# Neighbourhood attention in pairs: negated scores, keys in eight pieces, gate loads with the scores, two copies off ScalarE

## The chip, the cores and the metric

The kernel runs on one core of a Trainium2 chip. The metric is the device time of one execution in microseconds (us); three runs of the kernel before gave 1550.53, 1550.68 and 1553.64 us, so the median is 1550.68 us. All data are float32. Products use a split of one factor, or of both, into a high and a low part (`hh`/`hl`, `wh`/`wl`), each of which is kept in the form that the rows call fp32r.

## What is computed

There are two layers over 1024 latent tokens (a grid of 16 rows by 64 columns) and 256 context tokens, with 1024 features. Each layer normalises the input, projects it, runs three mixers side by side, multiplies each by a SiLU gate and projects back. The part that the change touches is the third mixer, attention of each grid row to a band of 8 rows and 16 columns, with a bias table, and to all context tokens:

```python
def row_block(r):
    r0 = jnp.clip(r - kh // 2, 0, rows - kh)
    ...
    s_nb = jnp.einsum("bqhd,bmqnhd->bhqmn", q_r, k_nb).astype(jnp.float32)
    bias = rpb[:, drow[:, None, None], dcol[None, :, :]]
    s_nb = s_nb + jnp.transpose(bias, (0, 2, 1, 3)).astype(jnp.float32)[None]
    s_ctx = jnp.einsum("bqhd,bchd->bhqc", q_r, k_ctx).astype(jnp.float32)
    s = jnp.concatenate([s_nb.reshape(bsz, NA_HEADS, GRID_W, n_nb), s_ctx], axis=-1)
    p = jax.nn.softmax(s, axis=-1).astype(v.dtype)
    ...
y = jnp.concatenate([a_out * silu(ag), b_out * silu(bg), n_out * silu(ng)], axis=-1) @ w_out[l]
```

The first mixer is attention of 8 heads over all tokens (grouped keys), the second a pooling mixer. In the first layer the context tokens also attend among themselves, with the heads of the first and of the third mixer.

## The kernel before, in words

A layer goes through these stages: projections (weights split on ScalarE and VectorE, products on TensorE, results written to DRAM as `qnd`, `knd`, `qad`, `kad`, gates as `ngd`, `agc`, `agd`); the **pair stage**, which the change is about; the global attention (lines 957 to 1139); the output projection (from line 1144). In the profiled execution the pair stage runs from about 398 to 523 us in the first layer and from about 1132 to 1237 us in the second.

The pair stage takes units of 128 queries and two heads (`pair_unit`, line 814). A neighbourhood unit (kind "n") of latent tokens has 4 or 5 tiles of 128 neighbourhood keys (`nk`) and two tiles of context keys; units of context queries ("n" with `nk` 0, and kind "c" for heads of the first mixer) have the two context tiles alone. The first layer has 28 units (two head pairs of 8 latent and 2 context units, then 8 "c" units), the second has 16. A unit has four steps:

- `scores(hi)` (line 823), for each of two heads: TensorE writes scores into one of two double banks `ps_w`. VectorE takes the maximum `m` over the 256 context columns (line 834), then one custom instruction adds the bias table in place and carries the maximum on (line 837; its accumulator is read by a second instruction). A small instruction negates the maximum into `nm` (line 841).
- `weights(hi)` (line 844): at the first head the unit's gate (64 KB, `ngate`) is loaded through SyncE's queue (line 847). ScalarE computes the exponential with bias `nm` and the row sum (line 852); VectorE takes the reciprocal `rr` (line 854); GpSimd multiplies the gate by it into `rg` (line 855).
- `transposes(hi)` (line 859), one unit later: TensorE transposes 128x128 blocks of the weights, four to a bank `ps_b` (three banks), at the second head also `rg` as the last block; ScalarE copies each bank to `probt` (line 870).
- `values()` (line 873), two units later: TensorE multiplies by the values (line 877), VectorE multiplies by the transposed gate into `una` (line 880), ScalarE copies that to `hh` (line 806), and GpSimd writes the rest to `hl` (line 807).

In one round of the loop at line 1086 the order on TensorE is: scores of head 0 of unit n, transposes of head 0 of unit n-1, scores of head 1, transposes of head 1, values of unit n-2. In the last 10 units of the first layer and the last 7 of the second, three products for the maxima of the global attention (`shift_step`, lines 985 and 990; they use the same three `ps_b` banks, and VectorE reduces each into `gmx`, line 986) stand in each round too.

TensorE's order is the program's (`manual_schedule`, line 97). On the other engines and on SyncE's queue a scheduler sets the order, by its own estimate of when things are ready; each engine then works its list in that order. All the loads and stores here go through SyncE's one queue.

The stage begins with the keys of the first head pair in `kst`. The keys of the second pair (`na_keys_load(1)`, line 901: four tiles, each loaded twice into halves of 64 partitions, eight transfers of 320 KB) are asked for together before unit 2; they go into `hh` and `hl`, and unit 10 (first layer) or 8 (second) is the first that reads them. `store_u` (line 803) is also used for the pooled branch (`fin`, line 811) and in the global attention.

Of the kernel before, what the change touches and what calls it, by code (L numbers as in the profile page):

```python
# [24 lines left out]
NTT = NT // P  # L25
HD = 64
EPS = 1e-6
NEG = -1e30
PB = 7
QB = 6  # L30

# [43 lines left out]
def hybrid_block_kernel(  # L75
# [84 lines left out]
    def load_gains():  # L160

        for i, g in enumerate((na_k_gain, att_k_gain, att_q_gain, na_q_gain)):
            for hf in range(2):
                SP.dma_start(out=gcol[hf * 64:(hf + 1) * 64, i, :], in_=g.rearrange("l d -> d l"))
        DVE.tensor_scalar(out=gcol[:, 2:4], in0=gcol[:, 2:4], scalar1=0.125, scalar2=None, op0=ALU.mult)

    hh = const.tile([P, KT, NT], F32R, name="hh")
    hl = const.tile([P, KT, NT], F32R, name="hl")
# [203 lines left out]
    for l in range(DEPTH):  # L372
# [391 lines left out]
        def na_table(h):  # L764

            T, I = tab_bufs[h % 2]
            for qr in range(2):
                off = RPB_PAD + (l * 4 + h) * RPB_H + (1 - qr) * 31 + 15
                SP.dma_start(out=T[qr * 64:(qr + 1) * 64],
                             in_=bass.AP(rpbd.tensor, rpbd.offset + off, [[RPB_S - 1, 64], [31, 14], [1, 64]]))  # L770
            DVE.tensor_tensor(out=T, in0=T, in1=cmask.unsqueeze(1).to_broadcast([P, 14, 64]), op=ALU.add)

        def na_inner(h):
            T, I = tab_bufs[h % 2]
            ACT.activation(out=I, in_=T[:, 2:12], func=AF.Copy)
            POOL.memset(I[0:64, 8:10], NEG)
            POOL.memset(I[64:128, 0:1], NEG)
            POOL.memset(I[64:128, 9:10], NEG)

        def load_nq(h, c0, n):  # L780
            t = ak_.tile([P, 512], F32R, name="nq", tag="q", bufs=QB)
# [5 lines left out]
        def na_keys_load(pr):  # L787

            places = [(hh[:, 2 + hi, :], hl[:, 2 + hi, :]) if pr else (kst(), kst()) for hi in range(2)]
            cur["k", pr] = [tuple(load_twice(places[hi][i], knd, 2 * pr + hi, 1 - i) for i in range(2)) for hi in range(2)]  # L790

        def na_q(pr, cc):
            cur["q", pr, cc] = [load_nq(2 * pr + hi, cc * 512, 512 if cc < 2 else 256) for hi in range(2)]

        na_keys_load(0)
        na_q(0, 0)
        for h in range(2):
            na_table(h)
# [4 lines left out]
        def store_u(f, t0, n, u, eng=DVE):  # L803

            dst = hh[:, f, t0:t0 + n]
            ACT.activation(out=dst, in_=u, func=AF.Copy)
            eng.tensor_tensor(out=hl[:, f, t0:t0 + n], in0=u, in1=dst.bitcast(F32), op=ALU.subtract)

        def pool_u(f, t0, n):
# [1 line left out]
            SP.dma_start(out=u[:, :n], in_=upd[f, :, t0:t0 + n])  # L811
            store_u(4 + f, t0, n, u[:, :n])

        def pair_unit(t, f, qs, ks, kbase, vs, k0, nk, tabs, gsrc):

            nl = nk * P
            base = 768 - nl
# [2 lines left out]
            st = _Env()  # L820
            st.s, st.p, st.pt = [None] * 2, [None] * 2, [None] * 2

            def scores(hi):
                q1, q2 = qs(hi)
                k1, k2 = ks[hi]
                S = ps_pair("ps_s")
                segs = [(base, k0 * P, 512 - base), (512, k0 * P + 512 - base, 256)] if nk else []
                segs.append((768, SEQ, 256))
                for o, kc, n in segs:
                    kc -= kbase  # L830
                    PE.matmul(S[:, o:o + n], q1, k1[:, kc:kc + n], start=True, stop=False)
                    PE.matmul(S[:, o:o + n], q2, k2[:, kc:kc + n], start=False, stop=True)
                m = small.tile([P, 1], F32, tag="m2", name="m2")
                DVE.reduce_max(out=m, in_=S[:, 768:1024], axis=AX.X)
                if nk:
                    m1 = small.tile([P, 1], F32, tag="m1", name="m1")
                    DVE.tensor_tensor_reduce(out=S[:, base:768], in0=S[:, base:768], in1=tabs[hi], scale=1.0, scalar=m,
                                             op0=ALU.add, op1=ALU.max, accum_out=m1)
                    m = m1
                nm = small.tile([P, 1], F32, tag="nm", name="nm")  # L840
                DVE.tensor_scalar(out=nm, in0=m, scalar1=-1.0, scalar2=None, op0=ALU.mult)  # L841
                st.s[hi] = S, nm

            def weights(hi):
                if hi == 0:
                    st.gate = ap_.tile([P, P], F32, name="ngate", bufs=3)
                    SP.dma_start(out=st.gate, in_=gsrc)
                    st.rg = ap_.tile([P, P], F32, name="rg", bufs=3)
                S, nm = st.s[hi]
                p = ap_.tile([P, 1024], F32, name="prob", tag="prob", bufs=PB)  # L850
                sm = small.tile([P, 1], F32, tag="sm", name="sm")
                ACT.activation(out=p[:, base:1024], in_=S[:, base:1024], func=AF.Exp, bias=nm, accum_out=sm)  # L852
                r = small.tile([P, 1], F32, tag="rr", name="rr")
                DVE.reciprocal(out=r, in_=sm)
                POOL.tensor_scalar(out=st.rg[:, hi * 64:(hi + 1) * 64], in0=st.gate[:, hi * 64:(hi + 1) * 64], scalar1=r,
                                   scalar2=0.0, op0=ALU.mult, op1=ALU.add)
                st.p[hi] = p

            def transposes(hi):

                p = st.p[hi]
                blocks = [p[:, base + i * P:base + (i + 1) * P] for i in range(nt)] + ([st.rg] if hi else [])
                pt = ap_.tile([P, 1024], F32, name="probt", tag="prob", bufs=PB)
                for i0 in range(0, len(blocks), 4):
                    part = blocks[i0:i0 + 4]
                    T = ps_one("ps_t")
                    for i, b in enumerate(part):
                        PE.transpose(T[:, i * P:(i + 1) * P], b, ident)  # L868
                    o = pt[:, i0 * P:(i0 + len(part)) * P]
                    ACT.activation(out=o, in_=T[:, :len(part) * P], func=AF.Copy)  # L870
                st.pt[hi] = pt

            def values():
# [16 lines left out]
        def early(i, fn):  # L890
            before.setdefault(max(i, 0), []).append(fn)

        order = [0, 1, 6, 7, 4, 5, 2, 3] + list(range(NTL, ntq))
        for pr in range(2):
# [33 lines left out]
        def make_unit(kind, pr, t):  # L928
            if kind == "n":
# [7 lines left out]
                else:  # L937
                    k0, nk, tb = 0, 0, None
                return pair_unit(t, 6 + pr, lambda hi: (qt[hi][:, ts_], qt[hi][:, ts_]), cur["k", pr], 0,
                                 lambda hi, kt: nv[:, kt, (2 * pr + hi) * 64:(2 * pr + hi + 1) * 64], k0, nk, tb,  # L940
                                 ngd[t, :, pr * P:(pr + 1) * P])
            f, g = pr, pr // 2
            cq = cur["cq", f]
            ts_ = slice((t - NTL) * P, (t - NTL + 1) * P)
            return pair_unit(t, f, lambda hi: (cq[hi][:, 0, ts_], cq[hi][:, 1, ts_]), [gk(g)] * 2, 0,
                             lambda hi, kt: av[:, kt, g * 64:(g + 1) * 64], 0, 0, None,
                             agc[t - NTL, :, f * P:(f + 1) * P])

        gks = {}

# [112 lines left out]
            early(len(units) - 12, gunits[i][4])  # L1063

        use_banks("pair")
        first = make_unit(*units[0])
        for hi in range(2):
            first[0](hi)
# [17 lines left out]
        for n, u in enumerate(units + [None, None]):  # L1086
# [17 lines left out]
            if p2:  # L1104
                p2[3]()
            prev = [fns, p1]
        shift_step(n_ahead - (n_all - len(shifts)))


# [147 lines left out]
def _constants():  # L1257
# [16 lines left out]
    mask = np.tile(np.where(okc, 0.0, NEG).astype(np.float32), (2, 1))  # L1274
    sel = np.zeros((P, 2), np.float32)
    for g in range(4):
        sel[32 * g, 0] = sel[32 * g + 1, 1] = 1.0
# [38 lines left out]
```

## Time and profile before

| | us |
|---|---|
| median of three runs | 1550.68 |
| profiled execution, its own time | 1550.23 |
| its span, first to last instruction | 1548.5 |
| pair stage, first layer | about 398 to 523 |
| pair stage, second layer | about 1132 to 1237 |

TensorE (PE) is busy in 1474.4 us, 95% of the span, VectorE (DVE) in 855.6, ScalarE (ACT) in 661.8, GpSimd (POOL) in 506.0. PE's busy time is modelled from pipelined instructions, so a stretch that reads as fully busy can still have slack. PEld is the loading of weights on TensorE, beside the products. The names that follow a line number are the program's buffers; SPq is SyncE's queue.

### The profile page before, as it was taken

To read this page: it belongs to the slowest core of one execution; us is meant where nothing else is said; L and a number is where in the kernel's file an instruction comes from. 1 tells how busy PE (TensorE), PEld (TensorE's weight loads), DVE (VectorE), ACT (ScalarE), POOL (GpSimd) and SP (SyncE) were. 2 spreads that over 40 slices of the span, in tenths; PEclk is the share of its full clock that TensorE was granted. 3 is DMA by queue.
4 is the path that set the end of the run, shared out by engine and by line. 5 is a ranking of instruction groups with operands and counts; after the bars stand their busy time and mean duration, and the time that the engine had idled before them with its cause. 6 is when DMAs were issued, how large, how long until landed. Compare 5 with 4: busy or idle time off the path is not lost.

```text
span 1548.5 us, 22305 instructions
## 1 busy us (share of the span) xinstructions
PE 1474.4 (95%) x8001; PEld 1074.7 (69%) x8001; DVE 855.6 (55%) x1721; ACT 661.8 (43%) x1296; POOL 506.0 (33%) x586
## 2 busy tenths in 40 slices
PE   5999999999899999998999999999989899999999
PEld 3787777788788555454788888878778754554577
DVE  3535234552477687875534444464357768786522
ACT  4543132333587544444322443332458544444400
POOL 0232336000132556566001132470013166565300
PEclk8999999999999999999999999999999999999999
DMA  9436455537746110101412223253696211001331
GB/s 306 148 98 219 128 157 164 165 103 191 169 123 167 45 42 21 41 7 41 176 55 104 87 79 104 76 149 83 174 218 158 79 31 41 22 21 41 120 132 55
DMA packets 153040, 167.91 MB, mean 108 GB/s; under 512 B 35384, under 2 KB 112032, under 8 KB 152864
## 3 DMA queue, kind: packets, MB, share of 16 engines
q1 hardware_dynamic: 152928, 166.48, 37.1%
q8 instruction: 63, 1.03, 0.3%
q14 instruction: 49, 0.40, 0.1%
HBM read 126.45 MB, written 40.86 MB: 108 GB/s over the span
## 4 chain that ended last, share of the span: by engine, by line
PE 52%; DVE 8%; ACT 3%; issue 2%; DMA 1%; POOL 1%; SPq 0%; DVEq 0%; ACTq 0%; POOLq 0%
PE ps_c L1031 7%; PE ps_w L1184 4%; PE ps_w L1187 4%; PE ps_w L1185 4%; PE ps_w L1011 4%; PE ps_w L1012 3%; PE ps_w L417 3%; PE ps_w L418 3%; PE ps_w L416 3%; PE ps_b L985 3%; DVE gt L1050 2%; DVE gmx L986 2%; PE ps_c L877 1%; DVE gacc L1022 1%; PE ps_w L426 1%
## 5 line engine op out<-in xcount | busy, mean ns | idle before, releaser
L1014 ACT ACTIVATE gp<-ps_w 128x1024 f32<-128x1024 f32 x160 | 162.4, 1022 | 183.5 <-PE ps_w L1012 147.2
L416 PE MATMUL ps_w<-wh,hh 128*128 128x512 f32 (+1 forms) x624 | 235.7, 378 | 1.7 <-ACT wh L285 1.7
L417 PE MATMUL ps_w<-wl,hh 128*128 128x512 f32 (+1 forms) x624 | 228.9, 367 | 0.3 <-DVE wl L286 0.2
L418 PE MATMUL ps_w<-wh,hl 128*128 128x512 f32 (+1 forms) x624 | 228.3, 366 | 0.0
L986 DVE TENSOR_REDUCE gmx<-ps_b 128x1 f32<-128x512 f32 x256 | 171.7, 685 | 75.7 <-PE ps_b L985 71.6
L1031 PE MATMUL ps_c<-gp,av 128*64 128x512 f32 x640 | 165.7, 611 | 10.4 <-ACT gp L1014 10.4
L1022 POOL TENSOR_TENSOR gacc<-gacc,gp 128x1024 f32<-128x1024 f32 x64 | 161.4, 2550 | 25.8 <-ACT gp L1014 25.5
L416 PEld LDWEIGHTS ps_w<-wh,hh 128*128 128x128 f32 x624 | 118.6, 190 | 26.8 <-issue 4.4
L418 PEld LDWEIGHTS ps_w<-wh,hl 128*128 128x128 f32 x624 | 117.9, 189 | 20.6
L417 PEld LDWEIGHTS ps_w<-wl,hh 128*128 128x128 f32 x624 | 118.1, 189 | 19.3 <-DVE wl L286 0.8
L1012 PE MATMUL ps_w<-gq,kst 128*128 128x512 f32 x320 | 126.2, 394 | 0.0
L1184 PE MATMUL ps_w<-woh,hh 128*128 128x512 f32 x272 | 109.1, 401 | 0.0
L1185 PE MATMUL ps_w<-wol,hh 128*128 128x512 f32 x272 | 107.1, 394 | 0.0
L637 DVE TENSOR_REDUCE qss<-sq 128x8 f32<-128x512 f32 (+2 forms) x58 | 31.1, 537 | 131.6 <-ACT sq L635 131.3
L1031 PEld LDWEIGHTS ps_c<-gp,av 128*64 128x64 f32 x640 | 42.7, 137 | 88.0 <-issue 65.7
L1019 POOL TENSOR_TENSOR gacc<-gp 128x1024 f32<-128x1024 f32 x32 | 75.8, 2368 | 50.7 <-ACT gp L1014 50.7
L286 DVE TENSOR_TENSOR wl<-wraw,wh 128x512 fp32r<-128x512 f32 (+1 forms) x96 | 66.5, 708 | 38.1 <-ACT wh L285 36.6
L1187 PE MATMUL ps_w<-woh,hl 128*128 128x512 f32 x272 | 85.0, 394 | 0.0
L852 ACT ACTIVATE prob<-ps_w,nm 128x768 f32<-128x768 f32 (+2 forms) x88 | 73.4, 834 | 21.9 <-DVE nm L841 16.6
L424 PE MATMUL ps_w<-hh,wh 128*128 128x512 f32 (+1 forms) x208 | 80.7, 388 | 0.9 <-ACT wh L285 0.9
L870 ACT ACTIVATE probt<-ps_b 128x512 f32<-128x512 f32 (+2 forms) x152 | 73.6, 532 | 17.1 <-PE ps_b L868 16.7
L635 ACT ACTIVATE sq<-ps_w 128x512 f32<-128x512 f32 (+2 forms) x58 | 27.9, 481 | 121.7 <-PE ps_w L418 121.7
(225 smaller groups left out, 2992.1 us busy)
## 6 DMA issues: line engine op xcount, KB each, us to landing
wmod<-in_w_mod_dram SPq DMA_DIRECT2D x48, 512.0 KB
wraw<-in_w_in_dram SPq DMA_DIRECT2D x64, 256.0 KB
gq<-qad SPq DMA_DIRECT2D x64, 128.0 KB
woraw<-in_w_out_dram SPq DMA_DIRECT2D x14, 512.0 KB
wraw<-in_w_in_dram SPq DMA_DIRECT2D x48, 128.0 KB
kst<-knd SPq DMA_DIRECT2D x16, 320.0 KB
qad<-qkhi SPq DMA_DIRECT2D x18, 256.0 KB
qad<-qklo SPq DMA_DIRECT2D x18, 256.0 KB
```

What stands on the lines that cost most here:

```text
L416: PE.matmul(ps[:, :n], a, wh[:, off:off + n], start=(k == 0), stop=False)
L417: PE.matmul(ps[:, :n], a, wl[:, off:off + n], start=False, stop=False)
L418: PE.matmul(ps[:, :n], b, wh[:, off:off + n], start=False, stop=(k == KT - 1))
L424: PE.matmul(ps[:, :n], wh[:, fs], hh[:, k, ts_], start=(k == 0), stop=False)
L986: DVE.reduce_max(out=mx[:, qt, half:half + 1], in_=S, axis=AX.X)
L1012: PE.matmul(S[:, i, :], k2[:, kc], st.q2[hi], start=False, stop=True)
L1014: ACT.activation(out=p, in_=S, func=AF.Exp)
L1022: eng.tensor_tensor(out=st.acc[hi], in0=st.acc[hi], in1=pf, op=ALU.add)
L1031: PE.matmul(st.o[hi * 64:(hi + 1) * 64, :], av[:, kt, g * 64:(g + 1) * 64], st.p[hi, kp][:, i, :], start=(kt == 0), stop=(kt == NTT - 1))
L1184: PE.matmul(ps[:, i2, :], a, oh[:, cs], start=(k == 0), stop=False)
L1185: PE.matmul(ps[:, i2, :], a, ol[:, cs], start=False, stop=False)
L1187: PE.matmul(ps[:, i2, :], b, oh[:, i2 * 512:(i2 + 1) * 512], start=False, stop=(k == KT - 1))
```

## The change

The sign of the neighbourhood scores is turned. The gain of `nq` is multiplied by -0.125 instead of 0.125, the bias table becomes mask minus bias with a mask of +1e30 outside, the reductions take the minimum, and the exponential has scale -1 and that minimum as its bias; so line 841 goes. For the "c" units (sign +1) the reduction itself negates its result. The keys of the second pair are asked for one transfer at a time, before units 1 to 8 in the first layer and before units 1, 1, 2, 3, 4, 4, 5 and 6 in the second. Except for the very first unit, the gate's load stands with `scores`, ahead of the products. The copy of the second bank of transposes at the second head moves from ScalarE to VectorE (this bank exists in the 32 units with `nk` 4 or 5: 3 or 4 blocks), and the copy of `una` to `hh` in all 44 units from ScalarE to GpSimd.

```diff
-NEG = -1e30
+FAR = 1e30
...
-        DVE.tensor_scalar(out=gcol[:, 2:4], in0=gcol[:, 2:4], scalar1=0.125, scalar2=None, op0=ALU.mult)
+        for i, v in ((2, 0.125), (3, -0.125)):
+            DVE.tensor_scalar(out=gcol[:, i], in0=gcol[:, i], scalar1=v, scalar2=None, op0=ALU.mult)
...
-            DVE.tensor_tensor(out=T, in0=T, in1=cmask.unsqueeze(1).to_broadcast([P, 14, 64]), op=ALU.add)
+            DVE.tensor_tensor(out=T, in0=cmask.unsqueeze(1).to_broadcast([P, 14, 64]), in1=T, op=ALU.subtract)
...
-            cur["k", pr] = [tuple(load_twice(places[hi][i], knd, 2 * pr + hi, 1 - i) for i in range(2)) for hi in range(2)]
+            cur["k", pr] = places
+            return [lambda hi=hi, i=i, r=r: SP.dma_start(out=places[hi][i][r * 64:(r + 1) * 64].bitcast(F32),
+                                                        in_=head(knd, 2 * pr + hi, 1 - i, slice(0, NT)))
+                    for hi in range(2) for i in range(2) for r in range(2)]
...
-            ACT.activation(out=dst, in_=u, func=AF.Copy)
+            if eng is POOL:
+                POOL.tensor_copy(out=dst, in_=u)
+            else:
+                ACT.activation(out=dst, in_=u, func=AF.Copy)
             eng.tensor_tensor(out=hl[:, f, t0:t0 + n], in0=u, in1=dst.bitcast(F32), op=ALU.subtract)
...
+            def load_gate():
+                st.gate = ap_.tile([P, P], F32, name="ngate", bufs=3)
+                SP.dma_start(out=st.gate, in_=gsrc)
+
             def scores(hi):
+                if hi == 0 and env.att:
+                    load_gate()
...
-                DVE.reduce_max(out=m, in_=S[:, 768:1024], axis=AX.X)
+                op = ALU.max if sign > 0 else ALU.min
+                DVE.tensor_reduce(out=m, in_=S[:, 768:1024], axis=AX.X, op=op, negate=sign > 0)
...
-                                             op0=ALU.add, op1=ALU.max, accum_out=m1)
+                                             op0=ALU.add, op1=ALU.min, accum_out=m1)
                     m = m1
-                nm = small.tile([P, 1], F32, tag="nm", name="nm")
-                DVE.tensor_scalar(out=nm, in0=m, scalar1=-1.0, scalar2=None, op0=ALU.mult)
-                st.s[hi] = S, nm
+                st.s[hi] = S, m
...
                 if hi == 0:
-                    st.gate = ap_.tile([P, P], F32, name="ngate", bufs=3)
-                    SP.dma_start(out=st.gate, in_=gsrc)
+                    if not env.att:
+                        load_gate()
...
-                ACT.activation(out=p[:, base:1024], in_=S[:, base:1024], func=AF.Exp, bias=nm, accum_out=sm)
+                ACT.activation(out=p[:, base:1024], in_=S[:, base:1024], func=AF.Exp, bias=nm, scale=float(sign), accum_out=sm)
...
-                    ACT.activation(out=o, in_=T[:, :len(part) * P], func=AF.Copy)
+                    if hi and i0:
+                        DVE.tensor_copy(o, T[:, :len(part) * P])
+                    else:
+                        ACT.activation(out=o, in_=T[:, :len(part) * P], func=AF.Copy)
...
-                early(s0 + 2, lambda: na_keys_load(1))
+                for i, fn in enumerate(na_keys_load(1)):
+                    early(s0 + 1 + i * (len(order) - 2) // 8, fn)
```

The order on TensorE is the same as before in the whole program. The lists of the other engines change in the two pair stages, and elsewhere only in single neighbours. Two places follow.

On SyncE's queue, at the start of the pair stage of the first layer, this stood before (`hh<-knd` and `hl<-knd` are the eight pieces of the second pair's keys, `agd<-itab` is the store of the last gate of the global attention, `fin` a piece of the pooled branch, `ngate` the gate of one unit):

```order
215 L753 DMA hh<-knd 64x1280
216 L847 DMA ngate<-ngd 128x128 x2
217 L753 DMA hh<-knd 64x1280
218 L753 DMA hl<-knd 64x1280 x2
219 L753 DMA hh<-knd 64x1280
220 L728 DMA agd<-itab_3596 128x512
221 L753 DMA hh<-knd 64x1280
222 L753 DMA hl<-knd 64x1280 x2
223 L811 DMA fin<-upd 128x512
224 L847 DMA ngate<-ngd 128x128 x2
```

and this stands there now (line numbers are those of the changed kernel: 793 the keys, 834 the gate, 820 `fin`, 730 the store):

```order
215 L793 DMA hh<-knd 64x1280
216 L834 DMA ngate<-ngd 128x128 x2
217 L793 DMA hh<-knd 64x1280
218 L820 DMA fin<-upd 128x512
219 L834 DMA ngate<-ngd 128x128
220 L793 DMA hl<-knd 64x1280
221 L834 DMA ngate<-ngd 128x128
222 L793 DMA hl<-knd 64x1280
223 L730 DMA agd<-itab_3597 128x512
224 L820 DMA fin<-upd 128x512
225 L834 DMA ngate<-ngd 128x128
226 L793 DMA hh<-knd 64x1280
```

The gates of units 2 and 3 stood behind the store and all eight pieces of the keys; they now stand ahead of the store, behind two and three pieces.

On VectorE, in one round late in the pair stage of the second layer (a unit with 5 neighbourhood tiles), this stood before (`m` the maxima, ISA the custom instruction and the reading of its accumulator, `gmx` the maxima for the global attention):

```order
1381 L834 TENSOR_REDUCE m_11732<-ps_w_10642 128x1
1382 L837 ISA ps_w_10642,m_11734<-ps_w_10642,itab_10456,m_11732 128x640
1383 L837 ISA m_11734 128x1
1384 L986 TENSOR_REDUCE gmx<-ps_b_69 128x1
1385 L841 TENSOR_SCALAR nm<-m_11734 128x1
1386 L834 TENSOR_REDUCE m_11765<-ps_w_10643 128x1
1387 L837 ISA ps_w_10643,m_11767<-ps_w_10643,itab_10458,m_11765 128x640
1388 L837 ISA m_11767 128x1
1389 L854 RECIPROCAL rr<-sm 128x1
1390 L986 TENSOR_REDUCE gmx<-ps_b_69 128x1
1391 L841 TENSOR_SCALAR nm<-m_11767 128x1
1392 L986 TENSOR_REDUCE gmx<-ps_b_70 128x1
```

and this stands there now (850 the minima, 853 the custom instruction, 885 the copy that was ScalarE's, 868 the reciprocal, 1004 `gmx`):

```order
1343 L850 TENSOR_REDUCE m_11649<-ps_w_10531 128x1
1344 L853 ISA ps_w_10531,m_11651<-ps_w_10531,itab_10345,m_11649 128x640
1345 L853 ISA m_11651 128x1
1346 L1004 TENSOR_REDUCE gmx<-ps_b_70 128x1
1347 L850 TENSOR_REDUCE m_11678<-ps_w_10532 128x1
1348 L853 ISA ps_w_10532,m_11680<-ps_w_10532,itab_10347,m_11678 128x640
1349 L853 ISA m_11680 128x1
1350 L868 RECIPROCAL rr<-sm 128x1
1351 L885 COPY probt<-ps_b_69 128x512
1352 L1004 TENSOR_REDUCE gmx<-ps_b_70 128x1
1353 L868 RECIPROCAL rr<-sm 128x1
1354 L1004 TENSOR_REDUCE gmx<-ps_b_71 128x1
```

The two negations are gone, so the exponential of a head waits for the accumulator itself and no longer for an instruction behind a `gmx`; the copy of the transposed bank stands between the first reciprocal and the second `gmx`.

## Rows read from the trace of the kernel before

**Rows 1.** Windows of the pair stages: busy us of each engine, granted clock, DMA.

```profile
core 0: us, PE busy (x) PEld busy (x) DVE busy (x) ACT busy (x) POOL busy (x), PEclk, DMA share, GB/s
410.00:420.00 10.00, 4.17 (x36) 3.71 (x36) 4.04 (x13) 5.66 (x13) 2.58 (x8) 0.73 1.00 224
1150.00:1160.00 10.00, 5.72 (x44) 5.27 (x45) 3.95 (x11) 4.67 (x11) 2.15 (x5) 0.83 1.17 232
...
424.62:489.03 64.41, 63.24 (x658) 57.17 (x658) 47.62 (x156) 57.45 (x135) 21.77 (x55) 1.00 0.54 145
489.03:522.31 33.28, 30.18 (x245) 21.50 (x245) 28.30 (x94) 21.18 (x71) 11.56 (x33) 1.00 0.39 109
1160.83:1181.04 20.21, 20.21 (x214) 18.68 (x213) 16.04 (x48) 18.26 (x41) 6.22 (x15) 1.00 0.63 161
1187.79:1227.80 40.01, 34.86 (x331) 30.55 (x330) 32.43 (x90) 26.42 (x56) 8.12 (x20) 1.00 0.34 95
```

**Rows 2.** Timeline of PE's value products, one group a round: start, us.

```profile
407.88 1.53 PE L877 MATMUL ps_c<-probt,nv 128*64 128x128 f32 x24
418.59 2.83 PE L877 MATMUL ps_c<-probt,nv 128*64 128x128 f32 x24
424.62 1.53 PE L877 MATMUL ps_c<-probt,nv 128*64 128x128 f32 x24
...
1145.51 1.53 PE L877 MATMUL ps_c<-probt,nv 128*64 128x128 f32 x24
1154.54 2.22 PE L877 MATMUL ps_c<-probt,nv 128*64 128x128 f32 x24
1160.83 1.53 PE L877 MATMUL ps_c<-probt,nv 128*64 128x128 f32 x24
1165.78 1.53 PE L877 MATMUL ps_c<-probt,nv 128*64 128x128 f32 x24
```

**Rows 3.** Timeline, first layer, 407 to 418 us; brackets give idle time and releaser.

```profile
407.56 0.33 SPq L728 DMA_DIRECT2D agd<-itab  x1
409.40 1.24 SPq L753 DMA_DIRECT2D hl<-knd  x2
411.31 0.90 SPq L847 DMA_DIRECT2D ngate<-ngd  x2
417.02 1.69 POOL L855 TENSOR_SCALAR rg<-ngate,rr 128x64 f32<-128x64 f32 x4 [4.13 <-DMA ngate<-ngd]
418.18 0.47 PE L868 MATMUL ps_b<-ident,rg 128*128 128x128 f32 x1 [5.83 <-POOL rg L855]
```

**Rows 4.** Chain that ended last, second layer: start, us, what.

```profile
1147.98 4.97 DMA ngate<-ngd
```

**Rows 5.** Timeline of one late round of the second layer.

```profile
1204.60 0.14 DVE L837 DVE_READ_ACCUMULATOR2_ANT m<- 128x1 f32 x1
1204.60 0.69 DVE L991 TENSOR_REDUCE gmx<-ps_b 128x2 f32<-128x512 f32 x1
1205.38 1.01 ACT L852 ACTIVATE prob<-ps_w,nm 128x896 f32<-128x896 f32 x1 [0.68 <-DVE nm L841]
1207.02 0.49 PE L985 MATMUL ps_b<-kst,hl 128*128 128x512 f32 x1 [1.00 <-ACT probt L870]
```

**Rows 6.** Instruction groups, whole program: count, busy us, mean ns, idle before.

```profile
L986 DVE TENSOR_REDUCE gmx<-ps_b 128x1 f32<-128x512 f32 x256 | 171.7, 685 | 75.7 <-PE ps_b L985 71.6
L841 DVE TENSOR_SCALAR nm<-m 128x1 f32<-128x1 f32 x88 | 13.0, 148 | 1.1
L806 ACT ACTIVATE hh<-una 128x128 fp32r<-128x128 f32 x44 | 14.0, 319 | 17.6 <-DVE una L880 17.5
L807 POOL TENSOR_TENSOR hl<-una,hh 128x128 fp32r<-128x128 f32 x44 | 21.4, 486 | 35.0 <-ACT hh L806 34.9
L855 POOL TENSOR_SCALAR rg<-ngate,rr 128x64 f32<-128x64 f32 x88 | 32.0, 367 | 141.4 <-DVE rr L854 35.2 <-DVE m L834 29.5 <-PE ps_b L868 20.6
```

**Rows 7.** A copy on VectorE from PSUM: ns min/median/max, place, shape.

```profile
L342 DVE COPY vcol<-ps_b x1: 191/191/191, 12.6 to 12.6; 128x40 f32<-128x40 f32 x1
```

More of the change, by code (lines that the diff above doesn't have):

```diff
@@ L775, in na_inner @@
             ACT.activation(out=I, in_=T[:, 2:12], func=AF.Copy)
-            POOL.memset(I[0:64, 8:10], NEG)
-            POOL.memset(I[64:128, 0:1], NEG)
-            POOL.memset(I[64:128, 9:10], NEG)
+            POOL.memset(I[0:64, 8:10], FAR)
+            POOL.memset(I[64:128, 0:1], FAR)
+            POOL.memset(I[64:128, 9:10], FAR)
         def load_nq(h, c0, n):
@@ L789, in na_keys_load @@
             places = [(hh[:, 2 + hi, :], hl[:, 2 + hi, :]) if pr else (kst(), kst()) for hi in range(2)]
-            cur["k", pr] = [tuple(load_twice(places[hi][i], knd, 2 * pr + hi, 1 - i) for i in range(2)) for hi in range(2)]
+            cur["k", pr] = places
+            return [lambda hi=hi, i=i, r=r: SP.dma_start(out=places[hi][i][r * 64:(r + 1) * 64].bitcast(F32),
+                                                        in_=head(knd, 2 * pr + hi, 1 - i, slice(0, NT)))
+                    for hi in range(2) for i in range(2) for r in range(2)]
         def na_q(pr, cc):
             cur["q", pr, cc] = [load_nq(2 * pr + hi, cc * 512, 512 if cc < 2 else 256) for hi in range(2)]
-        na_keys_load(0)
+        for fn in na_keys_load(0):
+            fn()
         na_q(0, 0)
@@ L812, in pool_u, with pair_unit @@
             store_u(4 + f, t0, n, u[:, :n])
-        def pair_unit(t, f, qs, ks, kbase, vs, k0, nk, tabs, gsrc):
+        def pair_unit(t, f, qs, ks, kbase, vs, k0, nk, tabs, gsrc, sign):
             nl = nk * P
@@ L940, in make_unit @@
                                  lambda hi, kt: nv[:, kt, (2 * pr + hi) * 64:(2 * pr + hi + 1) * 64], k0, nk, tb,
-                                 ngd[t, :, pr * P:(pr + 1) * P])
+                                 ngd[t, :, pr * P:(pr + 1) * P], -1)
             f, g = pr, pr // 2
@@ L946, in make_unit @@
                              lambda hi, kt: av[:, kt, g * 64:(g + 1) * 64], 0, 0, None,
-                             agc[t - NTL, :, f * P:(f + 1) * P])
+                             agc[t - NTL, :, f * P:(f + 1) * P], 1)
         gks = {}
@@ L1065, in hybrid_block_kernel @@
         use_banks("pair")
+        env.att = False
         first = make_unit(*units[0])
@@ L1106, in hybrid_block_kernel @@
             prev = [fns, p1]
+            env.att = True
         shift_step(n_ahead - (n_all - len(shifts)))
@@ L1273, in _constants @@
     okc = (col[None, :] >= c0[:, None]) & (col[None, :] < c0[:, None] + 16)
-    mask = np.tile(np.where(okc, 0.0, NEG).astype(np.float32), (2, 1))
+    mask = np.tile(np.where(okc, 0.0, FAR).astype(np.float32), (2, 1))
     sel = np.zeros((P, 2), np.float32)
```

## The prediction

> **What bounds the kernel now.** I read the windows of the two pair stages first, then the timeline of TensorE's value products (one group ends each round), then the chain of waits and the timeline around each long round. The windows show two stretches of 10 us in which TensorE is busy only 4.17 and 5.72 us, one in each layer, and the granted clock is 0.73 and 0.83 of full speed there, so partly at the lower of its two levels; no other stretch of the stages looks like that [rows 1]. The value products date the loss. From round to round an undisturbed stretch takes 4.95 us (1160.83 to 1165.78). In the first layer two rounds take 10.71 and 6.03 us (407.88, 418.59, 424.62), in the second 9.03 and 6.29 us (1145.51, 1154.54, 1160.83) [rows 2].
>
> The timeline names the cause. SyncE's queue issues the store of the last gate at 407.56, then the last pieces of the second pair's keys, and the gate of unit 2 only at 411.31. GpSimd waits 4.13 us for that gate, and TensorE 5.83 us for the product of gate and reciprocal, which it has to transpose before it can go on [rows 3]. In the second layer the chain itself runs through the same transfer, 4.97 us of it [rows 4]. So the loss is one of order on a queue: 64 KB stand behind half of 2.6 MB of keys that nobody needs for another six to eight units.
>
> Outside the two stalls three engines are close together. In the rounds of neighbourhood units without extra products ScalarE is busy 57.45 of 64.41 us and TensorE 63.24; where context units carry the products for the maxima VectorE leads with 28.30 of 33.28; in the late rounds of the second layer nobody is full (TensorE 34.86 of 40.01, VectorE 32.43) [rows 1], so there a chain through several engines sets the pace.
>
> **The change, part by part.** The sum is made against the profiled execution, 1550.23 us (span 1548.5, and 1.73 around it); that is 0.45 us under the median of 1550.68, which I neglect.
>
> *Keys in pieces, gates with the scores.* The bytes stay the same. What moves is that the gates of units 2 and 3 stand behind two and three pieces instead of eight, and ahead of the store that held the queue until 407.56. A gate is first needed at the second head's transposes one round later, so each now has a round or more to land. Both stalls should go: (10.71 - 4.95) + (6.03 - 4.95) = 6.84 us in the first layer, (9.03 - 4.95) + (6.29 - 4.95) = 5.42 in the second, together 12.3. The second round of each pair is counted because its slow products (2.83 us for 24 where 1.53 is usual) are the clock coming back after the idle stretch [rows 2]. Behind the earlier gates queue the later keys; the gate of unit 3 needs a buffer that GpSimd frees when unit 0 is done, so the queue waits there for about a round. The last piece still stands ahead of the gate of unit 8 in the first layer, and of unit 6 in the second, some two units before anyone reads it. The `fin` pieces also move ahead, and ScalarE and VectorE take them earlier in their lists; I cost that at nothing, since they are issued about two rounds before they are used.
>
> *The negation goes.* 88 instructions of 148 ns, 13.0 us of VectorE [rows 6]. What counts is where the exponential waits for it. In a late round of the second layer the accumulator is read from 1204.60 to 1204.74, a `gmx` stands next in VectorE's list, the negation behind it, and the exponential begins at 1205.38; ScalarE was idle 0.68 us for it. Behind the exponential come the copy of a transposed bank and the product that waits 1.00 us for that bank [rows 5], then the values and the next scores: a closed chain, round by round. With the negation gone the exponential can begin at about 1204.80, 0.58 us sooner. Seven rounds have this form: 4.1 us. In the first layer's last rounds VectorE leads; ten units drop 20 negations, 3.0 us at most, and less where the next instruction already overlaps: between 0 and 3.0 I take 2.
>
> *Two copies off ScalarE.* ScalarE loses 44 copies of 319 ns and, in 32 rounds, the copy of 3 or 4 transposed blocks. In the 14 rounds of rows 1's first long window and the 4 of the third this relieves the fullest engine but one. How much TensorE can use of it is bounded by its own rows: by its busy time the room is 64.41 - 63.24 plus nothing in the second layer, 1.2 us; by the loading of weights, busy 57.17 of 64.41 and 18.68 of 20.21, it is 8.8 us [rows 1]. I take 3, nearer to the lower end, because VectorE and the in-order lists keep some of it.
>
> Trainium Kernel Development and Optimization, the first page of the Trainium skill, says under Performance Expectations that the busy time of products is a bad measure of how near a kernel is to its limit, and that the loading of weights is a good one. The trace agrees in so far as the same 24 value products read as 1.53 us of busy time in one round and as 2.83 in another [rows 2]. By that rule alone the term would be 8.8 and the sum 27; by the busy time alone 1.2 and 19.6.
>
> *What is added.* 32 copies from PSUM on VectorE, 128x384 or 128x512. No row shows one of that size: a copy of 128x40 took 191 ns [rows 7], the reduction of 128x512 from PSUM 685 ns [rows 6]. I take 685, as the row of the same width and the same memory. In 14 rounds that is 9.6 us against 28 x 0.148 = 4.1 saved, and VectorE had 64.41 - 47.62 = 16.8 us idle there; in a late round 32.43/6 = 5.41 us of work become 5.41 - 0.30 + 0.69 = 5.80, against a new round of 40.01/6 - 0.58 = 6.09. So it is covered, narrowly in the second case. If the cover fails, 32 x 0.685 = 21.9 us could come back. The copies on GpSimd lie between 367 ns (the half as wide product with the reciprocal) and 486 (the subtraction of equal size) [rows 6]; 44 x 0.486 = 21.4 us stand beside an engine busy 21.77 of 64.41, and nobody but the output projection waits for them. The turned signs leave every other instruction as long as it was.
>
> The VectorE page of the Trainium skill (VectorE: DVE Perf Modes, Why PSUM operands drop a tier) states that a float32 copy from PSUM gets no faster mode, which speaks against the copies being cheap. No row here shows such a copy at this size; with the faster mode the term would be about half, and the sum would not move as long as VectorE is covered.
>
> Sum: 12.3 + 4.1 + 2 + 3 = 21.4; 1550.2 - 21.4 = 1528.8, say **1529**.
>
> **Rivals.** *A, only the stalls go.* TensorE's rows read 98 to 100% busy in the plain rounds, and VectorE's copies take back what the negation gives in the late ones: 1550.2 - 12.3 = 1538. For it: rows 1. Against it: the idle 0.68 and 1.00 us of rows 5. *B, a stall moves instead of going.* In the second layer the gate of unit 4 now stands behind the store, two more transfers of keys and `fin`, and five loads of 128 KB for the global attention, about 1.2 MB. If it lands too late, the second layer's 5.4 us come back: 1534. Against it: it is needed a round and a half after its issue. *C, slower.* The copy of the last bank waits for the transposed product of gate and reciprocal, which comes from VectorE's own reciprocal by way of GpSimd; before, ScalarE stood that wait, now VectorE's list does, and behind it stand the minima and the sum with the bias table of the next scores. With the copy (0.685) and a wait of 0.4 on the path in all 32 rounds, 34.7 us come, 9.5 for 64 negations and 12.3 for the stalls go: +12.9, 1563. It decides from (12.3 + 9.5)/32 = 0.68 us a round, so the bare copy on the path in every round would already cancel the gain. Against it: in rows 5 VectorE has time between its last `gmx` and the next scores. *D, more.* The plain rounds gain the whole 8.8 and the context rounds 3.0: 1550.2 - 12.3 - 4.1 - 3.0 - 8.8 = 1522.
>
> **How the numbers follow.** Forecast 0.54, A 0.20, B 0.10, D 0.07, C 0.09. A time within 0.2% of before (3.1 us, about what a measurement can tell) would come from a mild C, 0.04, and slower from the rest of it, 0.05; faster is 0.91. The range runs from 1519, a little under D for the rounds at the start of each stage, to 1543, above A by 5 us for `fin` pieces that arrive late or copies that are half uncovered. It leaves out C and the tails of the others, some 0.15.
>
> **What would show it.** Right: no slice of the pair stages below 0.9 of the clock, no wait of GpSimd for `ngate` above 1 us, value products 4.7 to 5.0 us apart where 10.71 and 9.03 stood, late rounds near 6.1 us, and the exponential waiting for the accumulator of line 853. Wrong: a new gap in the value products, a wait of TensorE for the product of gate and reciprocal, VectorE above 95% in the late rounds, or ScalarE waiting for `fin`.

## The result and the profile after

The changed kernel takes 1539.39 us (median of 4 runs, 1538.74 to 1541.54) against 1551.99 us for the kernel before beside it; the ratio is 0.9925, 95% interval 0.9913 to 0.9937. A second series gave 0.9913 (0.9897 to 0.9929). So it is 12 to 13 us faster: inside the range of the prediction (1519 to 1543), 10 us above its forecast (1529), with a little over half of the gain that was forecast (21.4 us).

The windows of the changed kernel first, in the order of [rows 1], with one more, the sixth, for a round that has no counterpart there:

```profile
core 0: us, PE busy (x) PEld busy (x) DVE busy (x) ACT busy (x) POOL busy (x), PEclk, DMA share, GB/s
401.00:410.00 9.00, 8.13 (x76) 7.13 (x75) 7.32 (x23) 8.13 (x19) 2.31 (x7) 1.00 0.87 219
1141.00:1150.00 9.00, 9.00 (x98) 8.52 (x98) 7.03 (x22) 7.63 (x17) 3.11 (x11) 1.00 1.01 236
415.58:479.82 64.24, 63.11 (x658) 57.18 (x657) 50.04 (x139) 49.89 (x109) 23.33 (x69) 1.00 0.56 146
479.82:512.67 32.85, 29.41 (x245) 21.71 (x245) 28.82 (x78) 18.34 (x58) 14.49 (x44) 1.00 0.52 149
1150.21:1160.12 9.91, 9.91 (x104) 9.23 (x103) 7.83 (x22) 7.61 (x16) 2.69 (x8) 1.00 1.18 213
1160.12:1168.13 8.01, 5.39 (x56) 4.86 (x56) 6.44 (x17) 6.47 (x15) 1.79 (x7) 1.00 0.35 98
1179.70:1217.09 37.39, 34.87 (x331) 30.54 (x330) 32.93 (x83) 22.11 (x45) 10.56 (x26) 1.00 0.31 88
```

The two idle stretches are gone and the clock holds there. The long plain stretch of the first layer holds the same 658 products and lasts 64.24 us where it was 64.41, although ScalarE is busy 7.56 us less in it. The context rounds went from 33.28 to 32.85, the six late rounds of the second layer from 40.01 to 37.39. One round of the second layer takes 8.01 us and TensorE is busy in 5.39 of them: a new wait.

The value products date it (start, duration; compare [rows 2]):

```profile
406.33 1.53 PE L894 MATMUL ps_c<-probt,nv 128*64 128x128 f32 x24
410.86 1.53 PE L894 MATMUL ps_c<-probt,nv 128*64 128x128 f32 x24
415.58 1.53 PE L894 MATMUL ps_c<-probt,nv 128*64 128x128 f32 x24
...
1140.95 1.53 PE L894 MATMUL ps_c<-probt,nv 128*64 128x128 f32 x24
1145.48 1.53 PE L894 MATMUL ps_c<-probt,nv 128*64 128x128 f32 x24
1150.21 1.53 PE L894 MATMUL ps_c<-probt,nv 128*64 128x128 f32 x24
...
1160.12 1.75 PE L894 MATMUL ps_c<-probt,nv 128*64 128x128 f32 x28
1168.13 1.75 PE L894 MATMUL ps_c<-probt,nv 128*64 128x128 f32 x28
```

The rounds of 10.71, 6.03, 9.03 and 6.29 us are now 4.53, 4.72, 4.53 and 4.73. The timeline of the new long round, instructions of four engines (brackets give idle time and what ended it):

```profile
1162.29 0.15 DVE L868 RECIPROCAL rr<-sm 128x1 f32<-128x1 f32 x1
...
1163.07 0.46 POOL L816 TENSOR_TENSOR hl<-una,hh 128x128 fp32r<-128x128 f32 x1
...
1165.85 0.73 ACT L777 ACTIVATE itab<-ntab 128x640 f32<-128x640 f32 x1
...
1166.64 0.20 POOL L778 MEMSET itab<- 64x128 f32 x1 [3.12 <-ACT itab L777]
...
1167.21 0.61 POOL L869 TENSOR_SCALAR rg<-ngate,rr 128x64 f32<-128x64 f32 x2
...
1167.87 0.33 PE L882 MATMUL ps_b<-ident,rg 128*128 128x128 f32 x1 [2.62 <-POOL rg L869]
```

Both reciprocals of unit 6 are there at 1162.44. GpSimd could form `rg` at 1163.5, but its list now has the fills of the next pair's bias table first, and these wait for ScalarE's copy of that table, which can't be written before unit 7 has read the old one. Nobody needs the table before unit 12. In the kernel before, GpSimd's list had both products of unit 6 ahead of the fills; the second of them and the first fill there:

```profile
1173.36 0.32 POOL L855 TENSOR_SCALAR rg<-ngate,rr 128x64 f32<-128x64 f32 x1 [0.59 <-DVE rr L854]
...
1176.31 0.20 POOL L776 MEMSET itab<- 64x128 f32 x1 [1.42 <-ACT itab L775]
```

So two of the prediction's own signs of being wrong have come: a new gap in the value products, and a wait of TensorE for the product of gate and reciprocal. The other two have not: VectorE is busy 32.93 of 37.39 us (88%) in the late rounds, and no wait of ScalarE for `fin` shows in either stage.

### The profile page after: what moved, and what is told of

The parts are those of the page before. It is cut to its first block, busy times and chain, and to the rows that moved or that the text cites. A ratio compares the mean times of both kernels' runs of the same rounds, so it can differ in the third digit from the quotient of the medians.

```text
span 1537.9 us, 22259 instructions
## 1 busy us (share of the span) xinstructions
PE 1474.2 (96%) x8001; PEld 1072.8 (70%) x8001; DVE 860.2 (56%) x1666; ACT 637.6 (41%) x1220; POOL 513.1 (33%) x630
## 4 chain that ended last, share of the span: by engine, by line
PE 80%; DVE 8%; ACT 4%; DMA 3%; issue 3%; SPq 1%; POOL 0%; DVEq 0%; POOLq 0%; ACTq 0%
PE ps_w L418 8%; PE ps_w L419 8%; PE ps_w L420 8%; PE ps_c L1049 8%; PE ps_w L1204 4%; PE ps_w L1207 4%; PE ps_w L1205 4%; PE ps_w L1029 4%; PE ps_b L1003 4%; PE ps_w L1030 3%; PE ps_c L894 3%; PE ps_b L882 2%; PE ps_w L426 2%; PE ps_w L428 2%; PE ps_w L427 2%
## 5 line engine op out<-in xcount | busy, mean ns | idle before, releaser
L866 ACT ACTIVATE prob<-ps_w,m 128x768 f32<-128x768 f32 (+2 forms) x88 | 72.7, 826 | 19.4 <-DVE m L853 7.4
L428 PE MATMUL ps_w<-hh,wl 128*128 128x512 f32 (+1 forms) x208 | 79.6, 382 | 0.0
L427 PE MATMUL ps_w<-hl,wh 128*128 128x512 f32 (+1 forms) x208 | 79.2, 381 | 0.0
```

## Experiments

Each row: ratio to the kernel before in the same series (95% interval), then from one profile the length of each layer's pair stage (first score product to first score of the global attention; 393.45 to 522.90 us in the first layer before) and the rest of the span. All figures in us.

```
run                 ratio [interval]          layer 1   layer 2   rest
before              -                          129.45    106.17   1312.9
changed             0.9925 [0.9913, 0.9937]    121.32     99.98   1316.6
changed again (e5)  0.9913 [0.9897, 0.9929]    121.26    101.55   1313.8
e1 keys, gates      0.9928 [0.9913, 0.9943]    123.17    101.98   1312.3
e2 sign             0.9980 [0.9969, 0.9990]    130.88    103.24   1310.5
e3 copies           1.0024 [1.0014, 1.0034]    132.44    107.69   1313.7
e12 sign, copies    0.9994 [0.9984, 1.0004]    129.69    104.38   1316.7
e6 no copies        0.9913 [0.9900, 0.9927]    123.03    101.21   1312.0
e7 una back         0.9905 [0.9890, 0.9920]    120.63    101.46   1312.8
e8 bank back        0.9919 [0.9906, 0.9931]    121.85    101.88   1313.5
e4 no fills         0.9898 [0.9882, 0.9914]    121.70    101.13   1311.2
e9 tied             0.9880 [0.9864, 0.9897]    120.61    100.32   1315.1
e10 tied, no fills  0.9895 [0.9880, 0.9910]    121.51    100.45   1312.0
e11 tied, una       0.9906 [0.9892, 0.9921]    121.93    100.08   1311.0
```

The rest, which the change does not touch, spans 6.2 us over these profiles. So a difference of 2 us between two profiles says nothing unless the stages show it.

**e1, keys and gates alone.** The diff keeps these edits of the change, and what they need:

```diff
+                for i, fn in enumerate(na_keys_load(1)):
+                    early(s0 + 1 + i * (len(order) - 2) // 8, fn)
...
+                if hi == 0 and env.att:
+                    load_gate()
```

> The kernel before with the keys in eight pieces and the gates loaded with the scores; signs and copies as before. Theory 1 (the two stalls are the whole of the large gain, and the new wait of the second layer comes from the same part): the first layer's stage ends 7.5 us earlier, the second gains 6.1 at its start and loses 2.6 to 3.1 at the change to the second pair, where GpSimd's list has the three fills of the bias table ahead of two products of gate and reciprocal; together 10.5 to 11 us, ratio 0.993. Theory 2 (the new wait comes from the copies that GpSimd took over): the new wait is absent, 13.6 us, ratio 0.991. Late rounds of the second layer stay at 6.6 to 6.7 us in both.

Ratio 0.9928: as much as the whole change. The first layer's stage is 6.3 us shorter, the second's 4.2. Of the new wait, 1.45 us are there (a round of 6.84 us): GpSimd waits 1.64 us at a fill ahead of the two products.

```profile
1161.69 0.20 POOL L776 MEMSET itab<- 64x128 f32 x1 [1.64 <-ACT itab L775]
...
1162.26 0.61 POOL L865 TENSOR_SCALAR rg<-ngate,rr 128x64 f32<-128x64 f32 x2
```

So the fills moved ahead with the keys, and theory 2 is out; the larger wait of the changed kernel does not come from the copies either, since e6, without them, waits 2.7 us. It comes with the turned sign, which is all that e6 has beyond e1; by what step is not shown. The late rounds stay at 6.71 us. The keys did it by themselves: with the gate's load moved alone, each engine's list in the built program is that of the kernel before, instruction by instruction, and with the keys alone that of e1. The scheduler already placed that load where it could; what held it was the block of keys.

**e2, the sign alone**, and **e3, the copies alone**:

```diff
-                nm = small.tile([P, 1], F32, tag="nm", name="nm")
-                DVE.tensor_scalar(out=nm, in0=m, scalar1=-1.0, scalar2=None, op0=ALU.mult)
```
```diff
+                    if hi and i0:
+                        DVE.tensor_copy(o, T[:, :len(part) * P])
...
+            if eng is POOL:
+                POOL.tensor_copy(out=dst, in_=u)
```

> The kernel before with the turned sign alone (no negation); keys, gates and copies as before. Theory 1 (the late rounds are shorter because the exponential no longer waits for a negation queued behind a maximum of the global attention): late rounds of the second layer 6.2 us instead of 6.67, 2.6 us, and about 0.5 in the first layer; both old stalls stay, 10.7 and 9.0 us. Together 3 us, ratio 0.998. Theory 2 (the late rounds are shorter because ScalarE lost two copies): late rounds stay at 6.6 us, ratio 1.000.

> The kernel before with the two copies moved alone (transposed second bank to VectorE, una to GpSimd). Theory 1: nothing where TensorE is full, ratio 1.000 within 1.5 us, ScalarE 7 us less busy in the first layer's plain rounds and their length unchanged. Theory 2: late rounds 6.2 us, 2.6 us gained, ratio 0.998. Theory 3 (the copy on VectorE delays the next scores' minima): 2 us or more lost in the late rounds, and the whole change would be better without it.

The sign alone gives 0.998: the late rounds are 6.10 us as in the changed kernel, the second layer's stage 2.93 us shorter. Its first stage is 1.4 us longer, which theory 1 did not have: in the first of two long rounds (6.49 and 5.49 us) ScalarE waits 2.27 us for a load of the output weights that stands in its list ahead of a bank of transposes.

The copies alone make the kernel slower, by 0.24%, and the late rounds stay at 6.71 us. Theory 2 is out. What theory 3 had wrong is the place: 3.0 of the 4.5 us that the stages lose are in the first layer. There ScalarE's waits for the negation grew (columns: total, times, longest; first the kernel before, then e3):

```profile
ACT prob L852 <- DVE nm L841: 9.0, 18, 1.0
...
ACT prob L855 <- DVE nm L844: 16.4, 30, 1.4
```

The timeline shows why: the copy stands ahead of the negation in VectorE's list.

```profile
472.77 0.67 DVE L874 COPY probt<-ps_b 128x512 f32<-128x512 f32 x1
...
473.36 0.14 DVE L844 TENSOR_SCALAR nm<-m 128x1 f32<-128x1 f32 x1
473.60 1.01 ACT L855 ACTIVATE prob<-ps_w,nm 128x896 f32<-128x896 f32 x1 [0.52 <-DVE nm L844]
```

**e12, sign and copies**, asks whether the cost goes with the negation (keys in one block at unit 2 and gates in `weights`, as before; the rest of the change kept).

> The kernel before with the turned sign and the two copies moved; keys in one block as before. Theory 1 (the copy on VectorE costs by standing ahead of the negation in VectorE's list, so the cost goes with the negation): as the turned sign alone, ratio 0.998, and ScalarE waits for the maximum no longer than 8 us in the first layer's stage. Rival (the copies cost 3.7 us whenever the keys come in one block, and it is the order of the keys that removes the cost): 0.998 x 1.0024 = 1.0004.

0.9994 lies between the two, and its interval overlaps that of e2, so the time does not decide. By its stages it equals the sign alone (234.07 us in both together against 234.12), and ScalarE waits 7.6 us for the maxima in the first layer, so the loss of e3 is gone there; but the ratio is 2.2 us worse than that of e2, and its profile is longer outside the stages. What that is stays open. The profile has 3.4 us more in the first layer's global attention than e2, with a clock of 0.83 to 0.84 in three of 22 slices of 10 us; e3 has about as much there (219.9 us), the changed kernel has not (217.0). The copies need not be its cause, since e6, without them, has 219.8 us too.

**e5 to e8, the changed kernel, and the same with copies put back** (e6 both, e7 that of `una`, e8 that of the bank):

```diff
-                    if hi and i0:
-                        DVE.tensor_copy(o, T[:, :len(part) * P])
-                    else:
-                        ACT.activation(out=o, in_=T[:, :len(part) * P], func=AF.Copy)
+                    ACT.activation(out=o, in_=T[:, :len(part) * P], func=AF.Copy)
```

> The changed kernel again, beside the next three. Both theories: ratio 0.9925 within its interval, 1538 to 1541 us; the round of 8.01 us at the change to the second pair is there again.

> The changed kernel with both copies back on ScalarE: keys in pieces, early gates and turned sign remain. Theory 1 (the copies cost 3.7 us only while the negation stood behind the copy in VectorE's list): no difference to the changed kernel beyond 1.5 us, ratio 0.992 to 0.9935. Rival (the parts add: 0.9928 x 0.998): ratio 0.9908, 2.6 us or more better than the changed kernel, so that the copies are a loss there too.

> The changed kernel with the copy of una back on ScalarE; the copy of the second bank stays on VectorE. Theory 1: within 1.5 us of the changed kernel. Rival: if the copies are a loss, this and the next run tell which of the two; a loss by GpSimd's copy shows here as 2 us less time than the changed kernel.

> The changed kernel with the copy of the second bank back on ScalarE; the copy of una stays on GpSimd. Theory 1: within 1.5 us of the changed kernel. Rival: a loss by VectorE's copy shows here as 2 us less time than the changed kernel.

All four intervals overlap; with both copies back the ratio is that of the changed kernel, 0.9913. Undisturbed rounds last 4.93 to 4.97 or 5.14 to 5.17 us with the copies on either side. So beside the ordered keys and without the negation, the copies change the time by nothing that these runs can tell, which is theory 1; the rival's 0.9908 lies in e6's interval too, but the gap of 2.6 us that it wanted to the changed kernel is 0.4 (1538.0 against 1538.42), and the stages are no shorter without the copies (224.2 us, against 221.3 and 222.8). By place they are not quite nothing. The first layer's long plain stretch takes 0.9 us more in e6 than in the changed kernel (64.24):

```profile
409.88:475.01 65.13, 63.28 (x658) 57.12 (x657) 44.95 (x128) 57.32 (x134) 21.09 (x55) 1.00 0.56 145
```

Against that, three late rounds of the second layer (6.63, 5.96 and 6.79 in the changed kernel) take 19.4 us together where the bank's copy is on VectorE (changed, e5, e7) and 18.7 where it is on ScalarE (e6, e8). There VectorE's list in the changed kernel has a `gmx` ahead of the custom instruction of the first head, the exponential comes late, and TensorE waits 1.30 us for a bank where e8 has 0.27:

```profile
1189.03 0.69 DVE L1004 TENSOR_REDUCE gmx<-ps_b 128x1 f32<-128x512 f32 x1 [0.27 <-PE ps_b L1003]
1189.64 0.75 DVE L853 CUSTOM_DVE_ANT_0 ps_w<-ps_w,ntab,m 128x512 f32<-128x512 f32 x1
...
1190.48 0.90 ACT L866 ACTIVATE prob<-ps_w,m 128x768 f32<-128x768 f32 x1 [0.98 <-DVE m L853]
...
1192.02 0.50 PE L1008 MATMUL ps_b<-kst,hh 128*128 128x256 f32 x2 [1.30 <-ACT probt L887]
```

**e4, no fills for the second pair**, aims at the new wait.

```diff
+            if h > 1:
+                ACT.activation(out=I[0:64, 0:8], in_=T[0:64, 2:10], func=AF.Copy)
+                ACT.activation(out=I[64:128, 1:9], in_=T[64:128, 3:11], func=AF.Copy)
+                return
```

> The changed kernel, but the second pair's inner bias tables are copied in two halves that leave the cells outside the band as the first pair's fills left them; GpSimd's fills of the second pair go. Theory 1 (GpSimd's list, with the fills waiting for ScalarE's copy of the table, is the new wait of 2.62 us of TensorE at 1165 us): the round of 8.01 us becomes 5.0 to 5.2, 2.9 us gained against the changed kernel, ratio to the kernel before 0.9906. Rival (the round is long because ScalarE's copy of the table and the pooled branch's piece delay the exponential): the round stays above 7 us, ratio 0.9925.

The round of 8.01 us becomes 5.17, as theory 1 has it, and the ratio (0.9898) has the number that it gave (0.9906) in its interval. Its sum is wrong all the same: the next rounds take 6.04, 7.57 and 7.59 us, where they took 4.94, 6.63 and 5.96, and the second layer's stage (101.13 us) lies between the two of the changed kernel (99.98 and 101.55). A match of the time alone would have passed for a proof.

**e9 to e11, the table's work tied to a later minimum** and asked for one unit later (e10: also without fills; e11: that, and `una` copied on ScalarE):

```diff
+                z = small.tile([P, 1], F32, tag="z", name="z")
+                DVE.tensor_scalar(out=z, in0=cur["m"], scalar1=0.0, scalar2=1.0, op0=ALU.mult, op1=ALU.add)
+            ACT.activation(out=I, in_=T[:, 2:12], func=AF.Copy, scale=z)
```

> The changed kernel; the copy of the second pair's inner tables (two for each layer) is multiplied by a one that VectorE makes from the newest minimum at the units that are two and three after the change of pairs, so that neither it nor GpSimd's fills can be listed earlier. Theory 1 (the long round at the change of pairs comes from fills listed ahead of two products of gate and reciprocal): the round of 8.01 us becomes 4.9 to 5.2, the next ones stay at 4.95, the second layer's stage takes 97 us instead of 100.0 to 101.6, ratio 0.989 to 0.990. Rival (the table's work costs the same wherever it stands): the long round goes and the late rounds take 1.5 us longer in all or more, ratio 0.9915.

> As the run before, and the table is copied in two halves without fills. Theory 1: as the run before within 1 us, since fills that nobody waits for cost nothing. Rival: the fills still hold a product of gate and reciprocal in a late round; then 1 us or more is gained against the run before.

> As the run before, with the copy of una back on ScalarE. Theory 1 (the two copies change nothing where the negation is gone): within 1.5 us of the run before. Rival (GpSimd's copy is a small loss, as 1537.2 against 1538.4 us in the earlier runs suggests): 1 us or more faster.

In all three the long round is 5.17 us and a later one grows to 7.1 to 7.7. The timeline of e9 shows what is late next: VectorE has the reduction for the global attention behind a reciprocal that waits for an exponential, and TensorE waits 2.03 us for that bank.

```profile
1174.56 0.19 ACT L871 ACTIVATION_READ_ACCUMULATOR prob<-ps_w,m 128x1 f32 x1
...
1174.86 0.16 DVE L873 RECIPROCAL rr<-sm 128x1 f32<-128x1 f32 x1 [1.13 <-ACT prob L871]
1174.93 0.67 DVE L1009 TENSOR_REDUCE gmx<-ps_b 128x1 f32<-128x512 f32 x1
...
1175.66 0.73 PE L1008 MATMUL ps_b<-kst,hh 128*128 128x512 f32 x2 [2.03 <-DVE gmx L1009]
...
1176.33 2.50 PE L899 MATMUL ps_c<-probt,nv 128*64 128x128 f32 x28
```

The same wait is 0.75 us in the changed kernel, where TensorE comes to it later. Behind the wait of e9 the granted clock falls as well (the value products above take 2.50 us where 1.75 is usual):

```profile
1178.00:1180.00 2.00, 2.00 (x14) 1.67 (x10) 1.08 (x4) 0.83 (x1) 1.11 (x4) 0.50 0.63 135
```

e4 and e10 have the same, a wait of 1.88 and 2.03 us and a slice at 0.50; e11 waits 1.44 us and its clock stays at 1.00. So theory 1 is right on the cause of the long round and wrong on what it is worth: it is waited for again one to three rounds on, and in three of the four kernels the clock adds to it. By the rounds the rival is nearer: in e9 the six late rounds take 38.83 us, 1.4 more than in the changed kernel, as it has it, and the two rounds ahead of them 1.6 more. By the ratio theory 1 is nearer. Neither e10 nor e11 is faster than the run before it (1536.32 and 1538.81 us against 1534.75 and 1536.32), so both their rivals fail; the differences are more than theory 1 allows, but the intervals overlap. The times of e4 and of e9 to e11 (0.9880 to 0.9906) are all at or below those of the changed kernel, and e9 is the fastest kernel here, 1534.75 us; e9's interval touches that of the second series of the changed kernel and lies below that of the first. Its profile, taken in its slowest run (1537.74 us), has stages 0.4 and 1.9 us shorter than the two of the changed kernel. Where the rest of its gain is, if it is one, is not shown.

## Why the prediction was right, and where it was not

*The stalls.* 12.3 us forecast; the four rounds gave 16.74 - 9.25 = 7.49 in the first layer and 15.32 - 9.26 = 6.06 in the second, 13.6 in all. The cause, the order on SyncE's queue, is shown by e1: this step was right. That the gates' new place was part of it is wrong: the keys alone do it. The 1.3 us more come from the yardstick: I took 4.95 us for an undisturbed round, and these last 4.53 to 4.73.

*The negation.* 0.58 us a round was right: 6.71 became 6.10. The late rounds' sum was 2.62 us where 4.1 was forecast, since one round grew (6.38 to 6.79) and the first (6.75 to 6.63), outside that window, hardly has this form. e2 shows it without the copies, and the accumulator, not an instruction behind a `gmx`, now releases the exponential (compare [rows 5]):

```profile
1196.31 0.14 DVE L853 DVE_READ_ACCUMULATOR2_ANT m<- 128x1 f32 x1
1196.31 0.69 DVE L1009 TENSOR_REDUCE gmx<-ps_b 128x2 f32<-128x512 f32 x1
...
1196.49 1.01 ACT L866 ACTIVATE prob<-ps_w,m 128x896 f32<-128x896 f32 x1
...
1198.13 0.51 PE L1003 MATMUL ps_b<-kst,hl 128*128 128x512 f32 x1 [0.40 <-ACT probt L887]
```

TensorE's wait for the bank is 0.40 us where it was 1.00. The context rounds gave 0.43, not 2: VectorE, which leads there, was not relieved. Its busy time reads 28.82 us where it was 28.30, although 18 negations are gone from the stretch; a copy of a bank and a subtraction for the output weights, 1.4 us together, now stand in it.

*The copies.* The step "I take 3, nearer to the lower end" failed: these rounds gained 0.17 us in the first layer and nothing in the two of the second that the new wait leaves alone. Against e6, which differs by the copies alone, it is 0.9 us. TensorE's busy time (98% of 64.41 us) fits as the bound: the same 658 products take 63.2 to 65.3 us in all kernels with the keys in order, and TensorE is busy 62.6 us or more of it. The rule on products' busy time that I cited from Trainium Kernel Development and Optimization (Performance Expectations), a page of the Trainium skill, would have given 8.8 us here; the measurement decides against that reading of it.

*What is added.* The durations (count, busy, mean ns):

```profile
L885 DVE COPY probt<-ps_b 128x512 f32<-128x512 f32 x16 | 10.8, 676 | 1.3 <-PE ps_b L1017 0.6 <-PE ps_b L882 0.6
L885 DVE COPY probt<-ps_b 128x384 f32<-128x384 f32 x16 | 8.7, 546 | 0.6 <-PE ps_b L882 0.6
L813 POOL CAST hh<-una 128x128 fp32r<-128x128 f32 x44 | 13.6, 310 | 31.1 <-DVE una L897 31.0
```

685 was right for the copy of 512 columns (676); the long plain stretch holds 13 of VectorE's copies with 8.06 us, where I reckoned 14 and 9.6. GpSimd's copy is cheaper than either bound of mine (310 against 367 to 486). VectorE's is covered but for 0.7 us in the late rounds, GpSimd's shows no cost. Rival C described a real mechanism, a copy in VectorE's list ahead of what the next exponential needs. e3 shows it in the first layer, beside the negation (16.4 us of waits); in the changed kernel ScalarE waits 6.8 us for the minima there, less than for the negation before (9.0).

*What is late next.* This is the other step that failed. I asked it of the queue (rival B: the gate of unit 4) and not of the other lists that the scheduler writes anew. That gate came in time; the fills did not let GpSimd use what was there. This cost 2.84 us in the first profile (8.01 against the 5.17 of that round in e4) and 4.4 in the second, where the round behind it was slow too. The parts make up the whole: the stages together gained 14.3 us in the first profile, and the parts above, less the 2.65 us by which the two rounds at the change of pairs grew (12.95 against 10.30 before), give 14.2. In the second profile the stages gained 12.8. The first profile lost 3.7 of its gain outside the stages, which there lie at the upper end of what all kernels show.

So the time of rival A (1538) came, and half of its reason: the plain rounds did stay as they were, but the late rounds did go faster, and the new wait took that back. The range held it because its upper end stood 5 us above A, for `fin` pieces that arrive late or copies that are half uncovered. Neither is what happened, so that much is luck.

## What to carry to other kernels

Small loads that gate a pipeline must not queue behind a large transfer that is needed much later; asking for its eight pieces one at a time instead of all at once was worth 11 us here, and moving the small ones in the program nothing. Where a scheduler writes the lists, read all of them after a change, most of all for work that is needed late and waits early (fills of a table, ahead of a product that others wait for). And judge an experiment by the stage that it aims at: e4 gave about the forecast time, while the stage that it was to shorten stayed as long as before.

## What the hardware showed

The same stall of TensorE cost two different amounts. In both profiles of the changed kernel it waits 2.62 us for `rg`. In the first the granted clock stays at 1.00 and the next round takes 4.94 us:

```profile
1166.00:1168.00 2.00, 0.13 (x1) 0.13 (x1) 1.10 (x2) 2.00 (x5) 1.04 (x5) 1.00 0.01 4
1168.00:1170.00 2.00, 2.00 (x30) 1.71 (x31) 1.37 (x3) 0.71 (x2) 1.04 (x5) 1.00 0.30 87
1170.00:1172.00 2.00, 2.00 (x19) 2.00 (x18) 1.35 (x4) 0.68 (x2) 0.75 (x2) 1.00 0.68 198
```

In the second the clock falls behind the wait, to 0.50 of full speed, its lower level, for a slice of 2 us, and the next round takes 6.51 us:

```profile
1162.00:1164.00 2.00, 0.00 (x1) 0.01 (x1) 1.23 (x5) 2.00 (x5) 1.04 (x5) 1.00 0.01 4
1164.00:1166.00 2.00, 2.00 (x25) 1.88 (x27) 1.29 (x2) 0.84 (x2) 0.96 (x5) 0.78 0.29 66
1166.00:1168.00 2.00, 2.00 (x14) 1.67 (x11) 0.29 (x1) 0.00 (x0) 0.82 (x3) 0.50 0.68 195
1168.00:1170.00 2.00, 2.00 (x17) 2.00 (x17) 1.24 (x3) 0.98 (x3) 0.00 (x0) 0.87 0.94 255
```

e6, e7 and e8 have the same wait (2.67, 2.63 and 2.75 us), slices at 0.50 to 0.53 behind it, and a next round of 6.29, 6.28 and 6.54 us. So in these five profiles a wait of this length cost itself alone once, and itself and 1.3 to 1.6 us more four times.
